# Computing the retention's k by features, with the weights standing, in a fused mixer and feed-forward kernel

## The chip, the cores and the metric

The kernel runs on one core of a Trainium2 chip. Its engines work side by side, each through its own queue in order: PE (TensorE, matrix products into the eight banks of PSUM), DVE (VectorE), ACT (ScalarE), POOL (GpSimd) and SP (SyncE, which issues most DMAs here). The metric is the device time of one execution in microseconds (us). The median of three executions of the kernel before is 429.26 us (429.15 to 429.53).

## The reference, cut to what matters

One layer of a model with 256 tokens of 1024 features. The input is modulated, `h = x * (1 + sc1) + sh1`, and one wide product makes every projection of the mixer:

```python
proj = h @ w_in
mq, mk, mv, rq, rk, rv, rg, g_a, g_r = jnp.split(proj, offsets, axis=-1)
mq = rotary_half(split_heads(mq, MOBA_HEADS), pos)
mk = rotary_half(split_heads(mk, MOBA_HEADS), pos)
y_a = moba_attention(mq, mk, split_heads(mv, MOBA_HEADS))
rq = retnet_rotate(split_heads(rq, RET_HEADS), pos)
rk = retnet_rotate(split_heads(rk, RET_HEADS), pos) * (RET_QK_DIM ** -0.5)
y_r = retention(rq, rk, split_heads(rv, RET_HEADS))
```

The retention has 4 heads of 128 features for q and k. Its rotation turns each pair of neighbouring features (2i, 2i+1) of a head by an angle that depends on the token:

```python
x0, x1 = xf[..., 0], xf[..., 1]
out = jnp.stack([x0 * cos - x1 * sin, x1 * cos + x0 * sin], -1)
```

Its scores are products of q and k over the 128 features of a head, so any order of these features does, if q and k have the same. After the mixer come two projections, a gate, an output projection, a layer norm, a feed-forward part with a short convolution, and a second layer norm.

## The kernel before, in words

PE works on numbers split into a high part (fp32r) and the rest, so that one product is three: high by high, high by low, low by high. Weights arrive from HBM as tiles of 128x2048 by SP's queue. Each half of such a tile, 128x1024, is split on the way: ACT copies it into `whi` (L1215) and DVE subtracts to make `wlo` (L1229). There are eight buffers of each.

The kernel begins with a phase A, which makes the modulated input `hh` (high) and `hl` (low, both by features: 128 features x 8 x 256 tokens) and, at the same time, the attention's q, k, v, the retention's q and one gate's first half, in all eight banks. `evac_A` (L966) moves these results out of the banks. Then comes a list of steps, one for each half tile of weights, carried out in order by the loop at the end of `_body`. In each step the loop first lets the side work go on (`run_sides`), then has the weights of up to six steps ahead split (`prep_to`), then carries out what was put off from an earlier step (`waiting`), and then issues the step's own matrix products. What stands in which order on an engine is settled by this loop when the program is written.

Three kinds of steps matter here. `xstat` (xh and xl stand in PE's array, the weights stream by): 12 products of 512 columns in a half tile, for two blocks of 128 tokens in two banks. Its result has tokens on the partitions. `wstat8m` (the weights stand, `hh` and `hl` side by side stream by): 8 products of 512 columns with `whi` (L116) and 8 of 256 columns with `wlo` (L118), into one bank; then ACT copies the bank's right half to SBUF (L448), and DVE, put off by one step, adds the left half to it (L451). Its result has features on the partitions. The third kind, `wstat4` and `wstat8`, also has weights standing.

The banks 0 to 3 go round: `two_banks` gives a pair in turn, `one_bank` the next one. Banks 4 to 7 belong to the side work: the attention and the retention.

The steps of the mixer are, in order: the retention's k (4 steps, `rk_done` L466), its v (8 steps), its gate (8), two other gates (4 and 8), two projections (4 and 8), then the output projection with banks 2, 3, 0, 1, 3 named in the code. Side by side with these, `mixers` (L980) ropes the attention's q and k (`rope`, L936, once for each block of tokens), turns them by features with PE's transposes and ACT's copies (`rot_T`, L957), and runs the attention head by head. It also ropes the retention's q and k, one of the four (block, q or k) per step (L1066), turns both by features (`rot_T`, L1072), and starts `retention` (L1074), which multiplies them (L1109, L1110).

## Time and profile before

| | |
|---|---|
| median of 3 executions | 429.26 us |
| the profiled execution, its own time | 428.88 us |
| its span in the profile | 427.2 us |
| PE busy | 415.9 us (97% of the span) |
| DVE busy | 373.4 us (87%) |
| ACT busy | 248.9 us (58%) |
| DMA, mean over the span | 247 GB/s |

The span is what the profile shows from the first to the last instruction; the execution's own time has 1.7 us around it. Busy shares are averages over the span. A matmul's end is modelled, so what a product costs is read from the distance between the starts of neighbours, not from its length.

### The profile page before, as it was taken

What the parts mean: (1) busy time and instruction counts of PE and PEld (TensorE: products, weight loads), DVE (VectorE), ACT (ScalarE), POOL (GpSimd) and SP (SyncE); (2) the same over time, 40 slices, a digit from 0 to 9 for tenths busy, and PEclk for the clock granted to TensorE, in tenths of its full rate; (3) what the DMA queues carried; (4) which work ended last, traced back from release to release, by engine and by line L of the source; (5) the groups of instructions that cost most, each with busy time, mean ns of one, the idle gap of its engine ahead of it and who ended that gap; (6) DMA issues with size and microseconds to landing.
All of it is one profiled execution on the core that took longest, in us unless ns stands there. A gap on an engine that the chain in (4) does not pass through costs nothing.

```text
span 427.2 us, 6209 instructions
## 1 busy us (share of the span) xinstructions
PE 415.9 (97%) x2316; PEld 357.2 (84%) x2316; DVE 373.4 (87%) x622; ACT 248.9 (58%) x404; POOL 7.3 (2%) x18
## 2 busy tenths in 40 slices
PE   6999999999999999999999999999999999999992
PEld 3888888877788998998889899888888888888882
DVE  5888999879997999999978887999999888789576
ACT  4667558779764488645543995654555545455400
POOL 0000000100000000001000000100000010000000
PEclk9999999999999999999999999999999999999998
DMA  7999988777468878789762075985875777550001
GB/s 261 407 412 396 399 284 358 275 291 298 164 242 327 284 262 297 296 295 353 283 202 98 2 275 219 348 288 192 296 276 216 292 284 235 189 192 1 2 25 74
DMA packets 19694, 105.61 MB, mean 247 GB/s; under 512 B 2640, under 2 KB 4560, under 8 KB 8912
## 3 DMA queue, kind: packets, MB, share of 16 engines
q1 hardware_dynamic: 18288, 100.23, 63.3%
q0 software_dynamic: 1376, 4.99, 3.3%
q8 instruction: 18, 0.29, 0.3%
q14 instruction: 12, 0.10, 0.1%
HBM read 104.15 MB, written 1.06 MB: 246 GB/s over the span
## 4 chain that ended last, share of the span: by engine, by line
PE 96%; DMA 1%; DVE 1%; SPq 1%; ACT 0%; issue 0%; DVEq 0%
PE P L116 22%; PE P L107 14%; PE P L108 13%; PE P L109 13%; PE P L118 12%; PE P L279 11%; PE P L289 3%; DMA raw<-in_strm 1%; PE P L674 1%; PE P L677 1%; PE P L676 1%; PE P L961 1%; PE P L1013 1%; PE P L1032 1%; PE P L1056 1%; PE P L1102 0%
## 5 line engine op out<-in xcount | busy, mean ns | idle before, releaser
L1229 DVE TENSOR_TENSOR wlo<-raw,whi 128x1024 fp32r<-128x1024 f32 x118 | 142.2, 1218 | 15.4 <-ACT whi L1215 15.0
L1215 ACT ACTIVATE whi<-raw 128x1024 fp32r<-128x1024 f32 x118 | 122.8, 1056 | 35.1 <-PE P L109 7.8
L206 DVE CUSTOM_DVE_ANT_0 junk<-raw,srow 128x1024 bf16<-128x1024 f32 x46 | 56.0, 1218 | 0.2
L116 PE MATMUL P<-AYa,whi 128*128 128x512 f32 x176 | 47.9, 394 | 0.0
L116 PE MATMUL P<-AYb,whi 128*128 128x512 f32 x176 | 47.2, 390 | 0.0
L107 PE MATMUL P<-whi,AH 128*128 128x512 f32 (+1 forms) x120 | 46.5, 388 | 0.0
L109 PE MATMUL P<-whi,AH 128*128 128x512 f32 (+1 forms) x120 | 45.2, 376 | 0.0
L108 PE MATMUL P<-wlo,AH 128*128 128x512 f32 (+1 forms) x120 | 45.1, 376 | 0.0
L116 PEld LDWEIGHTS P<-AYb,whi 128*128 128x128 f32 x176 | 33.0, 188 | 7.3
L448 ACT ACTIVATE A<-P 128x256 f32<-128x256 f32 x44 | 16.7, 380 | 34.9 <-PE P L118 32.9
L279 PE MATMUL P<-whi,AH 128*128 128x512 f32 x128 | 34.8, 394 | 0.4 <-ACT whi L263 0.4
L116 PEld LDWEIGHTS P<-AYa,whi 128*128 128x128 f32 x176 | 30.6, 190 | 4.3
L263 ACT ACTIVATE whi<-raw 128x1024 fp32r<-128x1024 f32 (+1 forms) x25 | 21.6, 883 | 17.6 <-DMA raw<-in_strm 16.4
L118 PEld LDWEIGHTS P<-AYa,wlo 128*128 128x128 f32 x176 | 26.9, 189 | 3.4
L266 DVE TENSOR_TENSOR wlo<-raw,whi 128x1024 fp32r<-128x1024 f32 (+1 forms) x25 | 24.6, 1010 | 5.3 <-ACT whi L263 5.1
L279 PEld LDWEIGHTS P<-whi,AH 128*128 128x128 f32 x128 | 23.5, 188 | 6.6 <-ACT whi L263 1.4
L118 PE MATMUL P<-AYb,wlo 128*128 128x256 f32 x176 | 28.3, 283 | 0.0
L118 PE MATMUL P<-AYa,wlo 128*128 128x256 f32 x176 | 28.0, 282 | 0.0
L107 PEld LDWEIGHTS P<-whi,AH 128*128 128x128 f32 x120 | 22.6, 188 | 5.0 <-issue 1.3
L109 PEld LDWEIGHTS P<-whi,AH 128*128 128x128 f32 x120 | 22.6, 188 | 4.3
L108 PEld LDWEIGHTS P<-wlo,AH 128*128 128x128 f32 x120 | 22.6, 189 | 3.6
L118 PEld LDWEIGHTS P<-AYb,wlo 128*128 128x128 f32 x176 | 24.3, 192 | 0.0
(277 smaller groups left out, 800.3 us busy)
## 6 DMA issues: line engine op xcount, KB each, us to landing
raw<-in_ada SPq DMA_DIRECT2D x16, 1024.0 KB, 5.5
raw<-in_wup SPq DMA_DIRECT2D x11, 1024.0 KB, 5.0
raw<-in_wgate SPq DMA_DIRECT2D x11, 1024.0 KB, 4.8
raw<-in_wdown SPq DMA_DIRECT2D x11, 1024.0 KB, 4.9
raw<-in_winB SPq DMA_DIRECT2D x10, 1024.0 KB, 6.9
raw<-in_strm SPq DMA_DIRECT2D x8, 1024.0 KB, 7.3
raw<-in_strm SPq DMA_DIRECT2D x12, 512.0 KB, 7.6
raw<-in_winGr SPq DMA_DIRECT2D x4, 1024.0 KB, 6.0
```

The costliest lines, as they stand in the source:

```text
L107: pe.matmul(o, lh, rh, start=start, stop=False)
L108: pe.matmul(o, lh, rl, start=False, stop=False)
L109: pe.matmul(o, ll, rh, start=False, stop=stop)
L116: pe.matmul(o, wh[:, k * 128:(k + 1) * 128], x2[k], start=k == 0, stop=False)
L118: pe.matmul(o[:, :256], wl[:, k * 128:(k + 1) * 128], x2[k][:, 0], start=False, stop=k == n - 1)
L206: dve.tensor_tensor_reduce(out=junk[:, rows], in0=raw[:, rows], in1=srow[:, rows], scale=1.0, scalar=0.0, op0=OP.mult, op1=OP.add, accum_o ...
L263: act.activation(hi[:, o], raw[:, o], AF.Copy)
L266: dve.tensor_tensor(lo[:, o], raw[:, o], f(hi[:, o]), OP.subtract)
L279: pe.matmul(pa[b0 + c // 512 * 2 + t], x[xi][:, j, t * 128:(t + 1) * 128], ws[k][:, c:c + 512], start=first and (xi, k) == (0, 0), stop=la ...
L448: act.activation(t, p[:, 256:], AF.Copy)
L1215: act.activation(hi, src, AF.Copy)
L1229: dve.tensor_tensor(lo, src, f(hi), OP.subtract)
```

## The change

The retention's k is made by two tiles of `wstat8m` in place of an `xstat`, from a weight tensor laid out for it (`winRk`). It is then by features from the start: for each head 128 features x 256 tokens, in the right half of the tiles `S["rqk", 0]` (heads 0 and 1) and `S["rqk", 1]` (heads 2 and 3). So k has four steps with one bank each (0, 1, 2, 3), and the turn of the banks comes out two banks on from there. Up to the first gate of the feed-forward part every step after k has the other pair of banks than before; at the first gate, `first` now sets the turn anew before the first half too, and from there the banks are the same as before.

The weights of the retention's q and k are permuted on the host within each head, even features first and then odd ones, so that the rotation's partners stand in two halves of 64 instead of side by side. `rope` loses its case for pairs: all ropes now use halves, the table of the sine has one half, and the sign is in a `scalar_tensor_tensor`. For k, features lie on partitions, so the partners lie 64 partitions apart: `k_swap` has ACT copy them across (two copies of 64x512 per block of two heads), and `k_rope`, one step later, does the rotation in three DVE instructions of 128x512 with a new table `kr` of 256 KB, loaded with the other constants. PE's transposes and ACT's copy for k are gone. In `mixers`, the attention's second block goes to banks 6 and 7 and not 4 and 5.

```diff
--- before.py
+++ after.py
...
-        for name, shape in (("cosm", [128, 2, 64]), ("sinm", [128, 2, 64]), ("mask", [128, 256]),
-                            ("cosr", [128, 2, 128]), ("sinr", [128, 2, 128]),
+        for name, shape in (("cosm", [128, 2, 64]), ("sinm", [128, 2, 32]), ("mask", [128, 256]),
+                            ("cosr", [128, 2, 128]), ("sinr", [128, 2, 64]),
                             ("convw", [128, 4, 22]), ("lncol", [128, 2, 8])):
             const(name, shape, sp)
+        consts["kr"] = slot("8b", [128, 4, 256])
+        sp.dma_start(consts["kr"][:, 0:2], a["kr"])
...
         def mk(half):
             def mm(hi, lo):
-                if half and mid:
-                    mid()
+                if mid:
+                    mid(half)
                 p = get()
...
-    def rk_done(bk):
-        for t in range(2):
-            act.activation(S["rqk", t][:, 512:1024], bk[t], AF.Copy)
-    xstat(None, "winB", 0, hh, hl, 8, lazy(two_banks), rk_done)
+    def rk_copy(half, u):
+        return S["rqk", u][:, 512 + half * 256:768 + half * 256]
+    for u in range(2):
+        wstat8m("winRk", u, lambda k: h1x2[:, :, k], lambda half, u=u: rk_copy(half, u), lambda half: None)
...
-        xstat(None, "winB", 2 + 2 * cc, hh, hl, 8, lazy(two_banks), rv_done)
+        xstat(None, "winB", 2 * cc, hh, hl, 8, lazy(two_banks), rv_done)
...
-        xstat(None, "winB", 6 + 2 * cc, hh, hl, 8, lazy(two_banks), rg_done)
+        xstat(None, "winB", 4 + 2 * cc, hh, hl, 8, lazy(two_banks), rg_done)
...
-    def first():
-        bank_i[0] = 0
-        up_T(1)
+    def first(half):
+        bank_i[0] = 2 - 2 * half
+        if half:
+            up_T(1)
     wstat8("wgate", 0, gh2, gl2, gate_done(0), first)
...
-    def rope(x, cos, sin, pairs):
-        n, w = cos.shape[-1], x.shape[-1]
-        heads = w // n
+    def rope(x, cos, sin):
+        w, h2, m = x.shape[-1], sin.shape[-1], cos.shape[-1]
+        n = 2 * h2
         t2 = slot("8a", [128, w])
-        hv = lambda t: t.rearrange("p (h n) -> p h n", n=n)
-        bc = lambda v, m: v.unsqueeze(1).to_broadcast([128, heads, m])
-        if pairs:
-            xv, tv = (hv(t).rearrange("p h (i two) -> p h i two", two=2) for t in (x, t2))
-            cv = sin.rearrange("p (i two) -> p i two", two=2)
-            for i in range(2):
-                dve.tensor_tensor(tv[:, :, :, i], xv[:, :, :, 1 - i], bc(cv[:, :, i], n // 2), OP.mult)
-        else:
-            h2 = n // 2
-            for i in range(2):
-                dve.tensor_tensor(hv(t2)[:, :, i * h2:(i + 1) * h2],
-                                  hv(x)[:, :, (1 - i) * h2:(2 - i) * h2],
-                                  bc(sin[:, i * h2:(i + 1) * h2], h2), OP.mult)
-        dve.tensor_tensor(hv(x), hv(x), bc(cos, n), OP.mult)
+        hv = lambda t, n: t.rearrange("p (h n) -> p h n", n=n)
+        bc = lambda v, k: v.unsqueeze(1).to_broadcast([128, w // k, v.shape[-1]])
+        for i in range(2):
+            o, y = hv(t2, n)[:, :, i * h2:(i + 1) * h2], hv(x, n)[:, :, (1 - i) * h2:(2 - i) * h2]
+            if i:
+                dve.tensor_tensor(o, y, bc(sin, n), OP.mult)
+            else:
+                dve.scalar_tensor_tensor(o, y, -1.0, bc(sin, n), op0=OP.mult, op1=OP.mult)
+        dve.tensor_tensor(hv(x, m), hv(x, m), bc(cos, m), OP.mult)
         dve.tensor_tensor(x, x, t2, OP.add)
+    def k_swap(x):
+        t2 = consts["kr"][:, 2:4].rearrange("p a b -> p (a b)")
+        for r in (slice(0, 64), slice(64, 128)):
+            act.activation(t2[r], x[64 - r.start:128 - r.start], AF.Copy)
+    def k_rope(x):
+        t = consts["kr"]
+        t2, xv = t[:, 2:4], x.rearrange("p (h t) -> p h t", h=2)
+        bc = lambda v: v.unsqueeze(1).to_broadcast([128, 2, 256])
+        dve.tensor_tensor(t2, t2, bc(t[:, 1]), OP.mult)
+        dve.tensor_tensor(xv, xv, bc(t[:, 0]), OP.mult)
+        dve.tensor_tensor(xv, xv, t2, OP.add)
...
-        roped = lambda i: rope(qk[i], consts["cosm"][:, i], consts["sinm"][:, i], False)
+        roped = lambda i: rope(qk[i], consts["cosm"][:, i], consts["sinm"][:, i])
...
-                    rot_T(qk[i - ROT_AT], i - ROT_AT, qkT, w, 4 + w)
+                    rot_T(qk[i - ROT_AT], i - ROT_AT, qkT, w, 4 + 2 * (i - ROT_AT) + w)
...
                 scores(i)
             if 0 <= i - RROPE < 4:
                 t, w = divmod(i - RROPE, 2)
-                rope(S["rqk", t][:, w * 512:w * 512 + 512], consts["cosr"][:, t], consts["sinr"][:, t], True)
+                x = S["rqk", t][:, 512:1024]
+                if w:
+                    k_rope(x)
+                else:
+                    rope(S["rqk", t][:, :512], consts["cosr"][:, t], consts["sinr"][:, t])
+                    k_swap(x)
             if 0 <= i - RROT < 2:
                 t = i - RROT
                 if t == 0:
-                    S["rT"] = [slot(n, [128, 4, 256]) for n in ("3a", "3b")]
-                for w in range(2):
-                    rot_T(S["rqk", t], t, S["rT"], w, 4 + 3 * w)
+                    S["rT"] = slot("3a", [128, 4, 256])
+                rot_T(S["rqk", t], t, [S["rT"]], 0, 4)
...
             if h < HR:
                 p = bank(4)
-                pe.matmul(p[:, 0:256], rT[1][:, h, 0:128], rT[0][:, h, :], start=True, stop=True)
-                pe.matmul(p[:, 256:384], rT[1][:, h, 128:256], rT[0][:, h, 128:256], start=True, stop=True)
+                o = 512 + h % 2 * 256
+                kr = S["rqk", h // 2][:, o:o + 256]
+                pe.matmul(p[:, 0:256], kr[:, 0:128], rT[:, h, :], start=True, stop=True)
+                pe.matmul(p[:, 256:384], kr[:, 128:256], rT[:, h, 128:256], start=True, stop=True)
...
-    cosm, sinm = lay(np.concatenate([c, c], 1)), lay(np.concatenate([-s, s], 1))
+    cosm, sinm = lay(np.concatenate([c, c], 1)), lay(s)
...
-    cosr, sinr = lay(np.repeat(c, 2, 1)), lay(np.stack([-s, s], -1).reshape(T, DK))
+    cosr, sinr = lay(np.tile(c, 2)), lay(s)
+    kr = np.stack([np.concatenate([c, c], 1).T, np.concatenate([-s, s], 1).T], 1)
...
-    return dict(cosm=cosm, sinm=sinm, cosr=cosr, sinr=sinr, decay=decay, mask=mask)
+    return dict(cosm=cosm, sinm=sinm, cosr=cosr, sinr=sinr, kr=kr, decay=decay, mask=mask)
...
-    wi = A(w_in)[0]
+    wi = A(w_in)[0].copy()
+    for c0 in (1536, 2048):
+        wi[:, c0:c0 + 512] = wi[:, c0:c0 + 512].reshape(-1, 4, 64, 2).transpose(0, 1, 3, 2).reshape(-1, 512)
...
-        winB=np.stack(sum([xs(wi, 2048 + 512 * i) for i in range(5)], [])),
+        winRk=np.stack([ws(wi, 2048 + 256 * i, 2) for i in range(2)]),
+        winB=np.stack(sum([xs(wi, 2560 + 512 * i) for i in range(4)], [])),
...
```

PE around the first step of the retention's v, before. P0 to P3 are banks of PSUM, `AH` holds `hh` and `hl`, `whi` and `wlo` are the split weights; the number behind a name tells one use of a buffer from the next.

```order
L108 MATMUL P1_718<-wlo_694,AH_123 128x512
L109 MATMUL P1_718<-whi_688,AH_123 128x512
L961 MATMUL P4_785<-ident_80,A2a_132 128x128 x4
L961 MATMUL P5_791<-ident_80,A2a_132 128x128 x4
L107 MATMUL P2_801<-whi_692,AH_123 128x512
L108 MATMUL P2_801<-wlo_700,AH_123 128x512
L109 MATMUL P2_801<-whi_692,AH_123 128x512
```

These are the last products of k (banks 0 and 1), the transposes of the attention's first block, and the first products of v, in bank 2, which nobody had used since phase A. The same place on PE in the changed kernel, from the first step of k:

```order
L116 MATMUL P0_719<-AH_123,whi_662 128x512 x8
L118 MATMUL P0_719<-AH_123,wlo_666 128x256 x8
L116 MATMUL P1_744<-AH_123,whi_664 128x512 x8
L118 MATMUL P1_744<-AH_123,wlo_670 128x256 x8
L116 MATMUL P2_767<-AH_123,whi_668 128x512 x8
L118 MATMUL P2_767<-AH_123,wlo_692 128x256 x8
L116 MATMUL P3_792<-AH_123,whi_690 128x512 x8
L118 MATMUL P3_792<-AH_123,wlo_696 128x256 x8
L974 MATMUL P4_810<-ident_80,A2a_132 128x128 x4
L974 MATMUL P5_816<-ident_80,A2a_132 128x128 x4
L107 MATMUL P0_827<-whi_694,AH_123 128x512
L108 MATMUL P0_827<-wlo_702,AH_123 128x512
```

The four steps of k now fill the banks 0 to 3 one after the other, and v's first product is in bank 0, the bank of k's first step. DVE in the same stretch of the program, before: `A2b` is the attention's second block, roped by L951 to L955, and the L1229 are the `wlo` of coming steps.

```order
L1229 TENSOR_TENSOR wlo_710<-raw_658,whi_702 128x1024
L951 TENSOR_TENSOR A8a_712<-A2b_133,sinm_644 128x16x32 x2
L954 TENSOR_TENSOR A2b_133<-A2b_133,cosm_642 128x1024
L955 TENSOR_TENSOR A2b_133<-A2b_133,A8a_712 128x1024
L1229 TENSOR_TENSOR wlo_733<-raw_658,whi_708 128x1024
L1229 TENSOR_TENSOR wlo_751<-raw_670,whi_731 128x1024
L1229 TENSOR_TENSOR wlo_767<-raw_670,whi_749 128x1024
```

And DVE there in the changed kernel, where L453 is the adding that frees a bank of k:

```order
L1248 TENSOR_TENSOR wlo_712<-raw_660,whi_704 128x1024
L952 SCALAR_TENSOR_TENSOR A8a_714<-A2b_133,sinm_644 128x16x32
L950 TENSOR_TENSOR A8a_714<-A2b_133,sinm_644 128x16x32
L953 TENSOR_TENSOR A2b_133<-A2b_133,cosm_642 128x1024
L954 TENSOR_TENSOR A2b_133<-A2b_133,A8a_714 128x1024
L1248 TENSOR_TENSOR wlo_739<-raw_660,whi_710 128x1024
L453 TENSOR_TENSOR AR0_675<-P0_719,AR0_675 128x256
L1248 TENSOR_TENSOR wlo_764<-raw_672,whi_737 128x1024
L453 TENSOR_TENSOR AR0_675<-P1_744,AR0_675 128x256
L1248 TENSOR_TENSOR wlo_787<-raw_672,whi_762 128x1024
```

The additions for banks 0 and 1 have come in behind the second block's rope and behind one and two more `wlo`; nothing else has moved in this stretch.

## Rows read from the trace of the kernel before

**Rows 1.** The page of the profile: the first line of its part 1 and the first line of its part 4 (the chain that ended last, by engine).

```profile
PE 415.9 (97%) x2316; PEld 357.2 (84%) x2316; DVE 373.4 (87%) x622; ACT 248.9 (58%) x404; POOL 7.3 (2%) x18
...
PE 96%; DMA 1%; DVE 1%; SPq 1%; ACT 0%; issue 0%; DVEq 0%
```

**Rows 2.** Who PE waited for in the whole span: us in total, times, longest.

```profile
PE P L191 <- DVE first L195: 3.2, 1, 3.2
PE P L279 <- ACT whi L263: 0.4, 1, 0.4
```

**Rows 3.** The timeline of PE from the first product of k: start, length, engine, line, operation, out<-in, count. L107 to L109 are an `xstat` step's products, L961 the transposes.

```profile
65.21 0.39 PE L107 MATMUL P<-whi,AH 128*128 128x512 f32 x1
...
75.86 0.39 PE L109 MATMUL P<-whi,AH 128*128 128x512 f32 x1
76.09 1.03 PE L961 MATMUL P<-ident,A2a 128*128 128x128 f32 x8
76.89 0.48 PE L107 MATMUL P<-whi,AH 128*128 128x512 f32 x1
...
78.34 0.39 PE L107 MATMUL P<-whi,AH 128*128 128x512 f32 x1
...
79.71 1.03 PE L961 MATMUL P<-ident,A2b 128*128 128x128 f32 x8
```

**Rows 4.** Pieces of the chain of waits in order of time: start, length, what. First the two groups of transposes of the retention's q and k (four of each in a group), then one half tile of a `wstat8m` step.

```profile
116.31 0.87 PE P L961 x8
...
121.22 0.87 PE P L961 x8
...
153.76 1.84 PE P L116 x8
155.60 0.95 PE P L118 x8
```

**Rows 5.** The timeline of DVE in the same stretch as rows 3: the first block's rope (L951 to L955, its middle left out), the `wlo` of coming steps, the second block's rope, and `wlo` again.

```profile
64.41 1.28 DVE L951 TENSOR_TENSOR A8a<-A2a,sinm 128x512 f32<-128x512 f32 x2
...
66.99 1.23 DVE L955 TENSOR_TENSOR A2a<-A2a,A8a 128x1024 f32<-128x1024 f32 x1
68.13 5.76 DVE L1229 TENSOR_TENSOR wlo<-raw,whi 128x1024 fp32r<-128x1024 f32 x5
73.81 1.28 DVE L951 TENSOR_TENSOR A8a<-A2b,sinm 128x512 f32<-128x512 f32 x2
...
76.39 1.23 DVE L955 TENSOR_TENSOR A2b<-A2b,A8a 128x1024 f32<-128x1024 f32 x1
77.53 5.76 DVE L1229 TENSOR_TENSOR wlo<-raw,whi 128x1024 fp32r<-128x1024 f32 x5
```

**Rows 6.** Groups of instructions by line and shape: count, busy us, mean ns of one, idle time before. L451 is the adding of a `wstat8m` step; L549 is a scalar_tensor_tensor with a number written in the instruction, L842 one with a scalar from a tile; L963 is ACT's copy of transposes.

```profile
L451 DVE TENSOR_TENSOR A<-P,A 128x256 f32<-128x256 f32 x44 | 18.3, 417 | 0.0
...
L549 DVE SCALAR_TENSOR_TENSOR A<-A2a,A8a 128x512 f32<-128x512 f32 x1 | 0.7, 693 | 0.0
L842 DVE SCALAR_TENSOR_TENSOR A7a<-A7a,sd,A 128x512 f32<-128x512 f32 x2 | 1.5, 740 | 0.0
L963 ACT ACTIVATE AYb<-P 128x512 f32<-128x512 f32 x4 | 2.5, 619 | 0.0
```

**Rows 7.** The timeline of ACT in the stretch of rows 3: the `whi` of coming steps, then one that waited for its weights.

```profile
66.66 6.88 ACT L1215 ACTIVATE whi<-raw 128x1024 fp32r<-128x1024 f32 x7
76.85 1.06 ACT L1215 ACTIVATE whi<-raw 128x1024 fp32r<-128x1024 f32 x1 [3.31 <-DMA raw<-in_winB]
```

**Rows 8.** The timeline of SP's queue: the last of the constants, and the next weights.

```profile
57.54 0.68 SPq L128 DMA_DIRECT2D lncol<-in_lncol  x1
61.51 11.60 SPq L96 DMA_DIRECT2D raw<-in_winB  x5
```

**Rows 9.** The timeline where the last `wstat8m` step of the mixer ends and the output projection begins: PE's last products of the former (four from 211.08 on), ACT's copy and DVE's adding that free its bank, and PE's first product for the second block of tokens.

```profile
211.08 0.64 PE L118 MATMUL P<-AYb,wlo 128*128 128x256 f32 x4
...
211.76 0.38 ACT L448 ACTIVATE A9b<-P 128x256 f32<-128x256 f32 x1 [0.94 <-PE P L118]
...
212.18 0.42 DVE L451 TENSOR_TENSOR A9b<-P,A9b 128x256 f32<-128x256 f32 x1
...
212.94 0.39 PE L107 MATMUL P<-whi,AH 128*128 128x512 f32 x1
```

**Rows 10.** Busy time of PE, PEld, DVE, ACT and POOL in three stretches, then the granted clock, the DMA share and GB/s: while ACT is fullest in the attention, and two stretches after PE's last matmul.

```profile
97.00:104.00 7.00, 7.00 (x39) 5.27 (x39) 6.86 (x22) 6.96 (x20) 0.00 (x0) 1.00 0.86 315
...
420.00:424.00 4.00, 0.00 (x0) 0.00 (x0) 3.86 (x11) 0.29 (x1) 0.00 (x0) 1.00 0.00 0
424.00:427.20 3.20, 0.00 (x0) 0.00 (x0) 0.37 (x1) 0.00 (x0) 0.00 (x0) 0.52 0.45 164
```

**Rows 11.** The timeline of PE at the start and the end of the kernel: its first eight transposes, the first product of phase A, and its last matmul.

```profile
3.23 1.94 PE L191 MATMUL P<-ident,sc 128*128 128x128 f32 x8 [3.23 <-DVE first L195]
...
8.85 0.50 PE L279 MATMUL P<-whi,AH 128*128 128x512 f32 x1 [0.42 <-ACT whi L263]
...
419.34 0.28 PE L109 MATMUL P<-whi,A 128*128 128x256 f32 x1
```

**Rows 12.** The timeline in the attention: ACT's copy of a head's transposed weights, and the products on PE that read it (of the pair's second head, in `A9b`).

```profile
109.20 0.49 ACT L1058 ACTIVATE A9b<-P 128x384 f32<-128x384 f32 x1 [0.89 <-PE P L1056]
...
111.86 0.43 PE L1032 MATMUL P<-A9b,A 128*64 128x256 f32 x1
```

## The prediction

> **What bounds the kernel now.** I read the page first: PE is busy 97% of the span and the chain that ended last is 96% PE [rows 1]. Then the view of waits, for PE alone: apart from the very start PE waited for nobody [rows 2]. So the time is the sum of what PE does, one thing after the other, plus a head and a tail. Whatever ACT, DVE and the DMAs do is free as long as PE finds its operands and an empty bank ready, and a new wait of PE counts in full. Two questions follow: how much PE work goes or comes, and whether PE, which waits nowhere now, will wait somewhere. For the second I read the timelines of PE, DVE and ACT side by side in the stretch where the change puts new instructions [rows 3, 5, 7].
>
> **PE's work.** k before: from 65.21 to 76.09, 10.88 us for 48 products [rows 3]. k after is four half tiles of a form that the kernel has elsewhere: 1.84 for eight products of 512 columns and 0.95 for eight of 256, so 2.79 a half [rows 4], 11.16 us in all. That is 0.28 more. The retention's transposes come in two groups of 0.87 for eight [rows 4]; half of each goes, 2 x 0.435 = 0.87 less. If nothing waited the sum would be 0.28 - 0.87 = -0.59 us.
>
> **The bank that v finds.** This is the step on which I rest the forecast. Before, v's first product went to bank 2, empty since phase A. After, it goes to bank 0, which held k's first half and is free only when ACT has copied its right half and DVE has added its left half. The copy is early: ACT has it behind the first five of the seven `whi` from 66.66 on, 0.98 us each, so at about 71.6, and k's first step on PE ends by 65.21 + 2.79 = 68.0 [rows 3, 7]. The addition is late. It stands on DVE behind the second block's rope and one more `wlo`, as the order shows, and DVE has no slack there: its instructions follow one another without a gap from 64.41 to 83.3 [rows 5]. So:
> - The second block's rope ended at 76.39 + 1.23 = 77.62, and the next `wlo` began at 77.53, since neighbours overlap a little [rows 5]. Two multiplications of 128x512, one per block, become scalar_tensor_tensors with a number in the instruction: 693 ns, against 1.28 for two of the old kind, whose single lengths with the overlap are some 0.68. I take +0.01 each; 740 ns is the other end, +0.06 each [rows 5, 6]. The `wlo` now begins at 77.55.
> - A `wlo` takes 5.76 / 5 = 1.15 from start to start [rows 5]: the addition for bank 0 begins at 78.70 and, at 417 ns [rows 6], ends at 79.12.
> - PE is at v's first product at 76.89 + 0.28 = 77.17 [rows 3]. It waits until 79.12 plus about 0.04 for the signal, which is what lay between a `whi` done and its first product at 8.85 [rows 11]; so 79.16, or 2.27 later than before.
> - The addition for bank 1 stands one `wlo` further on: 79.12 - 0.07 (overlap) + 1.15 + 0.42 = 80.62, or 80.69 without the overlap. PE's six products in bank 0 take 6 x 10.88 / 48 = 1.36 from 79.16, until 80.52. So PE waits again, by 0.1 to 0.2, and begins in bank 1 at about 80.7, where it began at 78.34 [rows 3].
> PE leaves this step 2.35 us later than before. The 0.28 of k's longer products lies inside that. Behind the waiting product on PE stand the rest of the step, the second block's transposes and all that follows; nobody ahead of PE makes it up, since PE was the bound already. The additions for banks 2 and 3 end some 3 us after that, and v comes to these banks only four steps on.
>
> **What else moves, and why I take it at nothing.** The four additions (1.67 us of DVE) delay the `wlo` of coming steps. But by 77.9 eleven `whi` have been made (three before evac_A, seven, and one) while PE begins its fifth half tile [rows 3, 7]: the weights are six steps ahead, and PE never waited for them [rows 2]. If that cover were gone it would cost the 1.67. `kr` adds 256 KB on SP's queue and the smaller tables take 96 KB off. SP was idle from 58.2 to 61.51, between the last constant and the next weights [rows 8], so the extra issue fits; 160 KB more at the page's mean of 247 GB/s is 0.65 us, and the `whi` that waits for its DMA until 76.85 [rows 7] is the eleventh, needed six steps later. `k_swap` gives ACT four copies of 64x512; the nearest row is 619 ns for 128x512 [rows 6], so 1.2 us in each of two steps, less two copies of transposes. They fall where ACT is 6.96 of 7.00 busy [rows 10]; I come back to this below. The ropes of q and k on DVE come out even: three instructions of 128x512 for k in place of four. The products of the retention itself keep their count and shape. In the output projection, bank 3 is now the bank of the last `wstat8m` half; the same copy and addition ended at 212.60 and PE came to its second bank at 212.94 [rows 9]. A slack of 0.3 us, so nothing to 0.1. The attention's second block in banks 6 and 7 can only remove a wait, and PE had none. From the feed-forward part on the banks are the same.
>
> **Sum.** +2.35 at v's first step, -0.87 of transposes: +1.48 us. Against the profiled execution's 428.88 that is 430.4; this execution lay 0.38 below the median of the runs shown, 429.26, so for the median I say 430.7.
>
> **Rivals.**
> 1. *The bank is free in time.* Then only PE's work counts: 429.26 - 0.59 = 428.7, not slower. Its place is the same addition, and it decides at PE's arrival, 77.17: DVE would have to be done with it 1.95 us earlier than by its rows. For it speaks only that the left half could be read early; against it that the order puts the addition behind a full row of work that cannot be shortened. 7 in 100.
> 2. *The clock falls while PE waits.* After PE's last matmul, at 419.6, the granted clock still read 1.00 up to 424 and 0.52 behind it [rows 10, 11]: of 2.4 GHz it fell to 1.2 only after an idle time of more than 4 us, and a wait of 2 us is shorter. At the start the low level shows in the transposes, 1.94 for eight against 1.03 [rows 3, 11], and PE's work from 3.23 to 8.85 would bound how long it stays low: half of 5.6 is 2.8 us more, 433.5. 5 in 100. The Trainium skill (TensorE: Matmul & The Clock Gate, section "A second HAM failure mode: psum-queue depth-cycling") says that PE pausing between groups of products, because of the turn of PSUM buffers, can make the clock swing between its two levels and cost throughput beyond the pauses. By that rule this would be the case to lose more than the wait; the trace has no pause of that kind in the middle, and its only row on the matter, the tail, speaks against it for a single pause.
> 3. *ACT or DVE run late in the attention.* The two copies of `k_swap` stand ahead of a `whi` and the next step's exponentials. If PE had to wait for them in full in both steps, that is 2 x 1.2 = 2.4 us, 433.1. But the narrowest place I find, a head's copy ended at 109.69 and read by PE at 111.86, has 2.2 us [rows 12], and ACT was waiting 0.89 just before that copy. PE is also 2.35 us later from the first wait on, which only helps. A part of it, up to 1 us, is the likelier form: 431.7. 9 in 100.
>
> **How the numbers follow.** The forecast case has 79 in 100, with its own range from 430.0 (DVE's stretch 0.5 us shorter than I count, and PE's gain a little larger) to 431.4 (740 ns for the new form, 0.3 at the output projection, a later signal). With the milder part of rival 3 I give 430.0 to 431.7 for 8 in 10. A difference of 0.2%, 0.86 us here, is about what a measurement of this kernel can tell from no change: slower begins at 430.12, faster ends at 428.40. The forecast case and the rivals 2 and 3 are slower, but for a low edge of the first, 0.88; rival 1 lies within 0.2%, and with that edge I give 0.09; faster would need rival 1 and some gain that I don't see, 0.03.
>
> **What would show it.** In the changed profile's waits, PE at L107 waiting for DVE's L453 (the addition on `AR`), twice, about 1.9 to 2.0 and 0.1 to 0.2 us. PE's first product of v at 79.1 to 79.2, where L118's last of k ends by 76.4. Groups of four transposes at the retention's two places, 0.43 each, and PE's busy share lower by about the wait. I am wrong if PE shows no wait there, if it is longer than 3 us, if the clock drops behind it, or if a second wait of more than 0.3 us stands in the attention or at the output projection.

## The result and the profile after

The changed kernel took 431.48 us (median of 7 executions, 430.88 to 433.66), the kernel before 429.4 beside it (429.15 to 430.4): a ratio of 1.0056, 95% interval 1.0042 to 1.007. The prediction was 430.7, range 430.0 to 431.7. The direction was right and the loss too small: +1.48 us was forecast, and +2.1 came, +2.4 by the ratio. This median lies inside the range, near its upper end. Two later sets of the same kernel on other occasions gave still more: 432.49 against 429.62 (1.0068, 1.005 to 1.0085) and 433.89 against 429.65 (1.0088, 1.0062 to 1.0114), and their medians lie 0.8 and 2.2 above the range.

The profiled execution of after took 431.52 us, its span is 429.8 (before: 428.88 and 427.2). First the page, the lines that answer to [rows 1], then PE's waits, which answer to [rows 2]:

```profile
PE 416.1 (97%) x2324; PEld 357.0 (83%) x2324; DVE 374.8 (87%) x624; ACT 250.6 (58%) x408; POOL 7.3 (2%) x18
...
PE 74%; DMA 11%; DVE 6%; ACT 5%; issue 2%; SPq 1%; DVEq 0%; ACTq 0%
```

```profile
PE P L193 <- DVE first L197: 3.2, 1, 3.2
PE P L107 <- DVE AR L453: 2.0, 1, 2.0
PE P L281 <- ACT whi L265: 0.7, 1, 0.7
PE P L281 <- ACT AH L250: 0.2, 1, 0.2
PE P L1069 <- ACT A9a L1071: 0.2, 1, 0.2
```

PE's busy share reads 97% as before, and says nothing. The chain does: it was 96% PE, and 22% of it now runs over DMAs, DVE and ACT. In the waits two rows are new behind the first stage: L107 for DVE's addition L453, the wait that the prediction rests on, and a small one for ACT, L1069.

PE's timeline, which answers to [rows 3] (L116 and L118 are a half of k, L974 the transposes, L107 to L109 v's products):

```profile
65.72 1.98 PE L116 MATMUL P<-AH,whi 128*128 128x512 f32 x8
...
76.87 1.04 PE L974 MATMUL P<-ident,A2a 128*128 128x128 f32 x8
79.86 0.50 PE L107 MATMUL P<-whi,AH 128*128 128x512 f32 x1 [1.95 <-DVE AR L453]
...
81.35 0.47 PE L107 MATMUL P<-whi,AH 128*128 128x512 f32 x1
...
82.81 1.03 PE L974 MATMUL P<-ident,A2b 128*128 128x128 f32 x8
```

And DVE's, which answers to [rows 5]:

```profile
62.74 1.28 DVE L986 TENSOR_TENSOR A2a<-P,A2a 128x512 f32<-128x512 f32 x2
...
68.86 5.76 DVE L1248 TENSOR_TENSOR wlo<-raw,whi 128x1024 fp32r<-128x1024 f32 x5
74.53 0.69 DVE L952 SCALAR_TENSOR_TENSOR A8a<-A2b,sinm 128x512 f32<-128x512 f32 x1
...
77.11 1.22 DVE L954 TENSOR_TENSOR A2b<-A2b,A8a 128x1024 f32<-128x1024 f32 x1
78.25 1.22 DVE L1248 TENSOR_TENSOR wlo<-raw,whi 128x1024 fp32r<-128x1024 f32 x1
79.39 0.42 DVE L453 TENSOR_TENSOR AR<-P,AR 128x256 f32<-128x256 f32 x1
79.72 1.22 DVE L1248 TENSOR_TENSOR wlo<-raw,whi 128x1024 fp32r<-128x1024 f32 x1
```

The two read together: PE has the transposes behind it at 77.9 and stands still until DVE, which has not had a free moment since 62.74, has done the second block's rope, one `wlo` and the addition. How much later PE is than before, at the same place of the program: 0.51 at k's start, 0.78 at its end (76.09 to 76.87), 2.97 at v's first product, 3.1 at the second transposes (79.71 to 82.81), 2.21 after both groups of the retention's transposes, which are four instead of eight, and 2.75 from 128 us on. The last step up, 0.54, is a loss that the sum had put at nothing, and PE's timeline shows it where the retention begins (L1056, then L1069, are the last head's transposes, L1109, then L1128, the retention's first product). Before and after:

```profile
124.47 0.39 PE L109 MATMUL P<-whi,AH 128*128 128x512 f32 x1
124.70 0.49 PE L1056 MATMUL P<-ident,A 128*128 128x128 f32 x3
125.03 0.60 PE L1109 MATMUL P<-AYa,AYb 128*128 128x256 f32 x2
...
125.60 0.48 PE L107 MATMUL P<-whi,AH 128*128 128x512 f32 x1
```

```profile
126.64 0.39 PE L109 MATMUL P<-whi,AH 128*128 128x512 f32 x1
127.19 0.55 PE L1069 MATMUL P<-ident,A 128*128 128x128 f32 x3 [0.16 <-ACT A9a L1071]
127.68 0.70 PE L1128 MATMUL P<-AYa,AR 128*128 128x256 f32 x2
...
128.35 0.48 PE L107 MATMUL P<-whi,AH 128*128 128x512 f32 x1
```

The transposes come 0.55 behind the start of the product ahead of them, where before it was 0.23, and from them to the next step's first product it takes 1.16, where before it was 0.90. What PE waits for is ACT, in ACT's timeline:

```profile
104.66 1.27 ACT L960 ACTIVATE A8b<-AR 64x512 f32<-64x512 f32 x2
...
113.74 1.28 ACT L960 ACTIVATE A8b<-AR 64x512 f32<-64x512 f32 x2 [0.64 <-DVE AR L968]
...
123.02 1.06 ACT L1234 ACTIVATE whi<-raw 128x1024 fp32r<-128x1024 f32 x1 [1.93 <-DMA raw<-in_winGa]
124.09 1.28 ACT L487 ACT_TABLE_LOAD   x1
...
126.62 0.51 ACT L1071 ACTIVATE A9a<-P 128x384 f32<-128x384 f32 x1
```

L960 are `k_swap`'s copies. The gate's weights were issued at 118.22, where before it was 114.18: 4.0 later, while PE was only some 3 later. SP's queue, before and after:

```profile
114.18 0.33 SPq L96 DMA_DIRECT2D raw<-in_winGa  x1
```

```profile
118.22 0.33 SPq L96 DMA_DIRECT2D raw<-in_winGa  x1
```

### The profile page after: what moved, and what is told of

Its sections match the earlier page's. It is cut to its first block, busy times and chain, and to the rows that moved or that the text cites. A ratio compares the mean times of both kernels' runs of the same rounds, so it can differ in the third digit from the quotient of the medians.

```text
span 429.8 us, 6226 instructions
## 1 busy us (share of the span) xinstructions
PE 416.1 (97%) x2324; PEld 357.0 (83%) x2324; DVE 374.8 (87%) x624; ACT 250.6 (58%) x408; POOL 7.3 (2%) x18
## 3 DMA queue, kind: packets, MB, share of 16 engines
HBM read 104.32 MB, written 1.06 MB: 245 GB/s over the span
## 4 chain that ended last, share of the span: by engine, by line
PE 74%; DMA 11%; DVE 6%; ACT 5%; issue 2%; SPq 1%; DVEq 0%; ACTq 0%
PE P L116 22%; PE P L118 12%; PE P L107 11%; PE P L108 11%; PE P L109 11%; DMA raw<-in_strm 8%; DVE wlo L1248 1%; DMA raw<-in_winB 1%; DVE wlo L268 1%; ACT whi L265 1%; DMA raw<-in_winGa 1%; ACT whi L1234 1%; PE P L677 1%; PE P L680 1%; PE P L679 1%
## 5 line engine op out<-in xcount | busy, mean ns | idle before, releaser
L116 PE MATMUL P<-AYa,whi 128*128 128x512 f32 x176 | 47.9, 394 | 0.0
L116 PE MATMUL P<-AYb,whi 128*128 128x512 f32 x176 | 47.2, 390 | 0.0
L107 PE MATMUL P<-whi,AH 128*128 128x512 f32 (+1 forms) x104 | 40.4, 388 | 2.0 <-DVE AR L453 2.0
L116 PEld LDWEIGHTS P<-AYb,whi 128*128 128x128 f32 x176 | 33.0, 188 | 7.3
L109 PE MATMUL P<-whi,AH 128*128 128x512 f32 (+1 forms) x104 | 38.9, 374 | 0.0
L108 PE MATMUL P<-wlo,AH 128*128 128x512 f32 (+1 forms) x104 | 38.9, 374 | 0.0
L116 PEld LDWEIGHTS P<-AYa,whi 128*128 128x128 f32 x176 | 30.6, 190 | 4.3
L118 PEld LDWEIGHTS P<-AYa,wlo 128*128 128x128 f32 x176 | 26.9, 189 | 3.4
L281 PEld LDWEIGHTS P<-whi,AH 128*128 128x128 f32 x128 | 23.5, 188 | 7.2 <-ACT whi L265 1.8
L118 PE MATMUL P<-AYb,wlo 128*128 128x256 f32 x176 | 28.3, 283 | 0.0
L118 PE MATMUL P<-AYa,wlo 128*128 128x256 f32 x176 | 28.0, 282 | 0.0
L107 PEld LDWEIGHTS P<-whi,AH 128*128 128x128 f32 x104 | 19.6, 188 | 6.7 <-DVE AR L453 2.4
L118 PEld LDWEIGHTS P<-AYb,wlo 128*128 128x128 f32 x176 | 24.3, 192 | 0.0
L116 PE MATMUL P<-AH,whi 128*128 128x512 f32 x96 | 24.2, 394 | 0.0
L109 PEld LDWEIGHTS P<-whi,AH 128*128 128x128 f32 x104 | 19.6, 188 | 3.6
```

What stands on the lines that cost most here:

```text
L107: pe.matmul(o, lh, rh, start=start, stop=False)
L108: pe.matmul(o, lh, rl, start=False, stop=False)
L109: pe.matmul(o, ll, rh, start=False, stop=stop)
L116: pe.matmul(o, wh[:, k * 128:(k + 1) * 128], x2[k], start=k == 0, stop=False)
L118: pe.matmul(o[:, :256], wl[:, k * 128:(k + 1) * 128], x2[k][:, 0], start=False, stop=k == n - 1)
L281: pe.matmul(pa[b0 + c // 512 * 2 + t], x[xi][:, j, t * 128:(t + 1) * 128], ws[k][:, c:c + 512], start=first and (xi, k) == (0, 0), stop=la ...
```

## The experiments

### The kernels once more

`again` and `again2` are the changed kernel, `before_again` is the kernel before.

> The changed kernel as it is, profiled and timed once more. First theory on the 0.5 us that the stage before k added (k's first product at 65.72 us instead of 65.21, with the same code ahead of it): it is scatter of that stage's transfers from run to run. Then the start of k moves by a few tenths between profiles of one kernel, and may come at 65.2 here. Rival: the change brings it (other transfers, other places in memory), and k starts at 65.6 to 65.8 again. For the time both expect 431.5 us, 430.9 to 433.7 in single runs.

Measured: 432.49 us (432.3 to 433.38), k's first product at 65.38.

> The kernel before, profiled once more, to see whether VectorE's row of additions at the end of the first stage stands at 62.0 us there as in the first profile, or moves. In the four profiles of changed kernels so far it begins at 62.7 to 63.3. Theory (scatter of that stage's transfers): it comes between 61.9 and 63.3 here, and k's first product at 65.2 to 65.9. Rival (the change brings it): 62.0 and 65.2 again. In both the product of v waits for nothing and the time is 428.7 to 430.9 us.

Measured: 430.45 us in its one execution. DVE's additions began at 63.75 (62.01 in the first profile of before) and k's first product at 65.91. In the timeline of PE, before then had a wait of its own, which the first profile did not have, and lost 0.9 there:

```profile
81.18 1.14 PE L961 MATMUL P<-ident,A2b 128*128 128x128 f32 x8 [0.62 <-ACT AYa L963]
```

So the first stage does scatter, in both kernels, and by more than was expected: 63.75 is 0.45 beyond the latest that the expectation had allowed. Over all 14 profiles of this study, whose first stage is the same code but for the tables among the constants, k's first product began between 65.15 and 66.22, with a median of 65.44; DVE's first addition of that stage's end between 62.01 and 63.75, with a median of 63.1. The profile on which the prediction rests had the earliest DVE of all.

`again` showed something else. In PE's timeline the products behind the pause are longer:

```profile
79.86 0.50 PE L107 MATMUL P<-whi,AH 128*128 128x512 f32 x1 [2.29 <-DVE AR L453]
80.20 0.48 PE L108 MATMUL P<-wlo,AH 128*128 128x512 f32 x1
80.48 0.63 PE L109 MATMUL P<-whi,AH 128*128 128x512 f32 x1
...
83.84 0.40 PE L108 MATMUL P<-wlo,AH 128*128 128x512 f32 x1
```

The busy times by stretch say why (the columns as in [rows 10]; the granted clock is the number ahead of the last two). First the profile of after, then `again`:

```profile
78.00:80.00 2.00, 0.14 (x1) 0.14 (x2) 2.00 (x4) 2.00 (x4) 0.71 (x1) 1.00 0.24 54
80.00:82.00 2.00, 2.00 (x9) 1.50 (x10) 2.00 (x3) 0.17 (x1) 0.00 (x0) 1.00 0.83 286
82.00:84.00 2.00, 2.00 (x15) 1.75 (x14) 2.00 (x4) 0.56 (x2) 0.00 (x0) 1.00 1.13 340
```

```profile
78.00:80.00 2.00, 0.14 (x1) 0.14 (x2) 2.00 (x4) 1.99 (x4) 0.59 (x1) 1.00 0.44 134
80.00:82.00 2.00, 2.00 (x6) 1.57 (x7) 2.00 (x3) 0.00 (x0) 0.00 (x0) 0.59 0.78 239
82.00:84.00 2.00, 2.00 (x6) 1.56 (x6) 2.00 (x4) 0.00 (x0) 0.00 (x0) 0.56 1.01 397
84.00:86.00 2.00, 2.00 (x15) 1.74 (x14) 1.33 (x2) 1.06 (x3) 0.35 (x1) 1.00 0.93 389
```

A granted clock of 0.5 is 1.2 of 2.4 GHz. PE started anew at the same 79.86 in both, but in `again` it was 1.5 later than after by 84 us, because the clock had fallen. That is rival 2, which the first profile had not shown. That profile does show that the row at the kernel's end, on which the prediction had set the rival aside, was one draw among many. In before the clock held for 4.5 us behind the end of the last product; in after it fell within 2 us:

```profile
422.08 0.28 PE L109 MATMUL P<-whi,A 128*128 128x256 f32 x1
```

```profile
424.00:426.00 2.00, 0.00 (x0) 0.00 (x0) 1.97 (x6) 0.29 (x1) 0.00 (x0) 0.57 0.00 0
```

### The banks of k

```diff
-                p = one_bank()
+                p = bank(at[half]) if at else one_bank()
...
+                ((2, 6), (7, 3))[u])
...
-                    rot_T(qk[i - ROT_AT], i - ROT_AT, qkT, w, 4 + 2 * (i - ROT_AT) + w)
+                    rot_T(qk[i - ROT_AT], i - ROT_AT, qkT, w, 4 + w)
```

> The changed kernel with k's four half products in banks 2, 6, 7 and 3 instead of 0 to 3, and the second pair of transposes back in banks 4 and 5: v's first pair 0 and 1 is then free from 64 us on. Theory (the wait for bank 0, 1.95 us, and the one for bank 1 behind it, 0.08, go into the end in full): the PE row that waits for DVE's addition is gone, and the time falls by 2.0, from 431.5 to 429.5 us. First rival (ScalarE and VectorE, late in the attention, set the pace anyway, and PE would only wait there instead): the wait at 79.9 us goes, the wait near 127 us grows from 0.54 to 1.5 or more, and the time falls by 1.0 or less, to 430.5 us or above. Second rival (another bank waits in its place, since k's halves now stand in the attention's banks): a new wait of 1 to 2 us between 68 and 90 us, and the time stays at 431 us.

Measured: 429.23 us (428.81 to 430.17), 0.9991 of the kernel before (0.998 to 1.0002), and 3.3 below `again` beside it. The wait is gone, and no other has come between 68 and 90 us; in PE's timeline v follows the transposes at once:

```profile
76.53 1.04 PE L975 MATMUL P<-ident,A2a 128*128 128x128 f32 x8
77.33 0.48 PE L107 MATMUL P<-whi,AH 128*128 128x512 f32 x1
```

k began at 65.39, as in `again` (65.38), so the two profiles can be set beside each other: the span is 427.1 against 431.2, and of these 4.1 PE has 2.5 at v's first product and 1.6 in the products behind it. The wait goes into the end in full, and with it what the clock took. Near 125 us PE still lost 0.47 here.

### The addition one place earlier, and one step later

`early` moves k's additions ahead of their step's `wlo` on DVE; `putoff2` puts them off by two steps.

```diff
-                put_off(1, rest)
+                (early if name == "winRk" else waiting).append((S["main"] + 1, rest))
...
+        while early and early[0][0] <= s:
+            early.pop(0)[1]()
         prep_to(max(need) + 1, True)
```

> The changed kernel with k's additions ahead of the subtraction of their step on VectorE instead of behind it: the first comes 1.14 us earlier, at 78.3 us, and the wait of PE for bank 0 falls to 0.8 to 1.3 us. Theory (time by the wait's length, and by the clock that falls behind the longer pauses): v's first product at 78.7 us, the granted clock stays 1.00 from 77 to 86 us, and the time falls by 1.14 from the runs without a fall (431.7), to 430.5 us, with single runs within 1 us of each other. Rival (the clock falls whatever the length of the wait): the median falls by 1.14 only from 432.4, to 431.3 us, and some profiles and runs still have 1.5 us more.

> The changed kernel with k's additions put off by two steps instead of one, so that VectorE has one more subtraction of 1.13 us (and the next addition's place) ahead of the first: it comes some 1.46 us later, and the wait of PE for bank 0 becomes about 3.4 to 3.9 us. Theory (PE waits by VectorE's clockwork alone, and what follows a pause of this length is a stretch of about 4 us at the lower clock level, granted 0.50 to 0.56, which costs 1.5 us more): PE goes on at 81.3 us, the granted clock falls in the profile and in nearly all runs, and the median is 1.5 above the longer runs of the changed kernel, 434.5 to 435 us. Rival (the falls of the clock at 80 us in two of three profiles have nothing to do with the pause's length): the clock falls in some runs only, and single runs spread from 433 to 434.7 us.

```diff
-                put_off(1, rest)
+                put_off(2 if name == "winRk" else 1, rest)
```

Measured: `early` 431.02 us (430.33 to 432.77), the clock 1.00 from 76 to 88 us in its profile; `putoff2` 435.38 (433.8 to 436.78), the clock 0.60 and 0.55 from 80 to 84. The two rows of PE's timelines, `early` first:

```profile
79.36 0.50 PE L107 MATMUL P<-whi,AH 128*128 128x512 f32 x1 [1.72 <-DVE AR L453]
```

```profile
80.50 0.77 PE L107 MATMUL P<-whi,AH 128*128 128x512 f32 x1 [2.97 <-ACT whi L1234]
```

`early` was forecast with a pause of 0.8 to 1.3 and v at 78.7, and had 1.72 and 79.36. The step of 1.14 was there, but from a later start: DVE's first addition stood at 63.38. Its time lies between the 430.5 and the 431.3 that were expected and settles nothing between them. Its single runs spread by 2.4 us and not by 1, so more than this profile shows happens in some of them. In `putoff2` the row names a `whi` on ACT, which ended at 80.48; DVE's addition had ended at 80.35, so up to 0.1 of the pause is ACT's. Its v came only 0.64 later than in after, since its DVE began at 62.14, the second earliest of all; counted from there it is 1.24, against 1.46 forecast.

All kernels with the pause, by their profiles (us; the clock is that granted from 82 to 84):

| kernel | DVE's first addition | v's first product | apart | pause named | clock |
|---|---|---|---|---|---|
| after | 62.74 | 79.86 | 17.12 | 1.95 | 1.00 |
| again | 62.74 | 79.86 | 17.12 | 2.29 | 0.56 |
| again2 | 63.70 | 80.82 | 17.12 | 2.41 | 0.50 |
| dveswap | 62.87 | 79.98 | 17.11 | 2.38 | 0.69 |
| filler | 63.51 | 80.63 | 17.12 | 1.20 | 1.00 |
| early | 63.38 | 79.36 | 15.98 | 1.72 | 1.00 |
| putoff2 | 62.14 | 80.50 | 18.36 | 2.97 | 0.55 |

The fourth column is the point: in the five kernels with the same order on DVE, v begins 17.11 to 17.12 us after DVE's first addition, so it begins when DVE has gone through a fixed row of work. PE's own start of k, which lay between 65.34 and 66.22 in these profiles, changes nothing in that.

### The pause filled

```diff
+                if i == ROT_AT:
+                    p = bank(6)
+                    for _ in range(8):
+                        pe.matmul(p, hh[:, 0, 0:128], hh[:, 0:2].rearrange("p a b -> p (a b)"),
+                                  start=True, stop=True)
```

> The changed kernel with eight products of 128x512, which nothing reads, into bank 6 behind the first transposes: PE works for 8 x 0.23 = 1.84 us of the time in which it would stand still before v's first product, and the wait for bank 0 stays what VectorE makes it. Theory (what comes on top of the wait in some runs is the lower clock level behind a pause of more than about 2 us): v's first product at 79.9 us as before, a remaining idle of 0.1 to 0.7, the granted clock 1.00 from 76 to 88 us, and the median falls from that of the changed kernel beside it (432.4 in both sets so far) by about 0.7, to that of its runs without a fall, 431.6 us. Rival (the clock falls there for another reason, or the fall costs the median nothing): median as the changed kernel's, or the clock low again at 80 us.

> The changed kernel once more, beside the one with the pause filled, on the same chip: 431.5 to 432.5 us by both theories. If the pause before v's first product is over 2.2 us in the profile, the theory of the clock expects a granted clock of 0.5 to 0.6 from 80 to 84 us; if it is under 2.0 us, 1.00.

Measured: `filler` 433.54 us (433.47 to 433.82), `again2` 433.89 (431.67 to 435.17). The clock behaves as the theory has it: 1.00 throughout with the pause filled, 0.50 behind the 2.41 of `again2`, and the runs of `filler` lie within 0.35 us of each other where those of `again2` spread by 3.5. The median does not: it should have been 431.6. In `filler` v began at 80.63, 0.7 above the forecast's 79.9, and PE lost 1.8 near 125 us instead of 0.5, since there the gate's weights landed 6.1 us after their issue (4.8 in after). ACT's timeline shows what that cost it:

```profile
125.11 1.06 ACT L1239 ACTIVATE whi<-raw 128x1024 fp32r<-128x1024 f32 x1 [3.23 <-DMA raw<-in_winGa]
```

So the fall makes the changed kernel's runs spread; what it adds to the median is not shown by this. Why the weights were slow here is not settled either.

The granted clock averaged over each run's span, which the record has for every run, says more. Of the 19 runs of the changed kernel in its three sets, the nine at 0.994 or above took 430.88 to 432.38 us, with a median of 431.5, and the ten at 0.993 or below 432.12 to 435.17, with a median of 433.5. Of these ten, two are among the seven of the first set, three among the six of `again` and five among the six of `again2`, which is the order of the three medians. Where PE has no pause, in `banks`, the clock orders nothing: its three runs at 0.994 or below took 428.9 to 429.8, the others 428.81 to 430.17. The average also counts the clock behind the last product, which costs nothing, so it can't show where in a run the clock fell.

### ScalarE's copies of the partners

Five kernels take them away. `dveswap` and `both` (with the banks turned) let DVE multiply across the halves of the partitions:

```diff
-            act.activation(t2[r], x[64 - r.start:128 - r.start], AF.Copy)
...
-        dve.tensor_tensor(t2, t2, bc(t[:, 1]), OP.mult)
+        for r, o in ((slice(0, 64), slice(64, 128)), (slice(64, 128), slice(0, 64))):
+            sn = t[o, 1].unsqueeze(1).to_broadcast([64, 2, 256])
+            dve.scalar_tensor_tensor(t2[r], xv[o], -1.0, sn, op0=OP.mult, op1=OP.mult)
```

> The changed kernel with the four copies of ScalarE for k's partners gone: VectorE multiplies the partners across the two halves of the partitions itself, in two instructions of 64x512 instead of one of 128x512. ScalarE loses 4 x 0.63 = 2.5 us between 104 and 115 us and no longer waits for the one partner buffer (0.64); VectorE gets one instruction more for each token half, some 0.7 us each. The wait for bank 0 stays. Theory (the loss of 0.54 us at 127 us comes from ScalarE, made late by those copies): PE loses 0.1 or less there, and the time falls by 0.5, to 431.0 us. Rival (that loss has another cause, VectorE's work or the load of the gate's weights): PE still loses 0.4 to 0.6 there and the time stays at 431.5 us, or rises by up to 0.7 with VectorE's longer work.

> The two edits together: k's halves in banks 2, 6, 7 and 3, and the partners multiplied by VectorE without ScalarE's copies. Theory (the wait for bank 0 and ScalarE's lateness are the two losses, and they add): 431.5 - 2.0 - 0.5 = 429.0 us, which is 0.4 below the kernel before (429.4), the 0.59 of PE work that the change saves less what the first stage scatters. Rival (they are one loss: once PE no longer waits at 79.9, ScalarE's lateness has another size): no better than the edit of the banks alone, 429.5 us.

Measured: `dveswap` 432.88 us (431.52 to 435.1), `both` 428.8 (428.55 to 429.8), 0.9985 of before (0.9974 to 0.9995), which is not clear of the banks alone. Near 125 us PE lost 0.37 and 0.36, not 0.1. That much of the theory fell. Two instructions of 64x512 take DVE 1.39 where one of 128x512 took 0.69, so DVE now brought the delay that ScalarE had brought, which the runs further down bear out.

`banks_dma` swaps by transfers on POOL's queue, with the banks turned:

```diff
-            act.activation(t2[r], x[64 - r.start:128 - r.start], AF.Copy)
+            nc.gpsimd.dma_start(t2[r], x[64 - r.start:128 - r.start])
```

> The banks edit (k's halves in banks 2, 6, 7, 3) and the swap of k's partners by two transfers on the queue of POOL for each token half, in place of the two copies of ScalarE. VectorE's work is that of the changed kernel (0.69 for the one multiplication of 128x512), ScalarE loses 4 x 0.63 = 2.5 us. In the edit of the banks alone PE loses 0.47 us near 125 us behind ScalarE's copies (VectorE waits 1.06 for ScalarE at 107 us, the load of the gate's weights is issued 1.37 late); with VectorE's own swap it lost 0.36, where VectorE had 0.7 us more work for each token half. Theory (each of the two lost there by its own engine's extra work, and with none on either engine the loss goes): PE loses 0.1 or less near 125 us, and the time is 0.4 below the edit of the banks alone: 428.8 us, 0.7 to 0.9 below the kernel before. Rival (the loss comes from k's rope being in another place, or the transfers come late and VectorE waits for them): 0.3 to 0.5 lost again, 429.2 us or above.

Measured: 430.27 us (428.71 to 431.09), worse than the banks alone; PE lost 1.2 near 125 us. The time was the rival's, the way was not: DVE waited for no transfer. POOL's queue was empty, so the first pair went out at 82.58, into the fullest stretch of the weights; it took 9.2 us to land, and ACT stood still for weights issued right behind it, 4.67 against 1.54 with the banks alone:

```profile
92.53 1.06 ACT L1235 ACTIVATE whi<-raw 128x1024 fp32r<-128x1024 f32 x1 [4.67 <-DMA raw<-in_winB]
```

`banks_noswap` leaves the copies out and puts nothing in their place:

```diff
-        dve.tensor_tensor(t2, t2, bc(t[:, 1]), OP.mult)
+        dve.tensor_tensor(t2, xv, bc(t[:, 1]), OP.mult)
...
-                    k_swap(x)
```

> The banks edit with k's partner copies left out and nothing in their place: k is multiplied by its own rows where the partners belong, so the retention's result is another one, but VectorE's instructions, shapes and order are those of the edit of the banks, and no transfer is added. Theory (with the banks turned, what PE still loses near 125 us, 0.47, is ScalarE's copies, which hold up L87's copy and with it VectorE by 1.06, and so the gate's weights): VectorE waits 0.2 or less there, PE loses 0.1 or less at 125 us, and the time is 0.4 below that of the banks alone: 428.8 us. Rival (the loss comes from the transfers' scatter in that stretch, as it did when two more transfers were put there): 0.3 or more lost, 429.2 us or above.

Measured: 428.44 us (428.13 to 429.24), 0.9972 of before (0.9962 to 0.9982). PE loses nothing near 125 us. From the last head's transposes to the next step's product it is 0.90 again, as before the change:

```profile
123.98 0.49 PE L1065 MATMUL P<-ident,A 128*128 128x128 f32 x3
...
124.88 0.47 PE L107 MATMUL P<-whi,AH 128*128 128x512 f32 x1
```

With the copies in, DVE shows the way they take, in its timeline of `banks`:

```profile
107.18 0.42 DVE L88 TENSOR_TENSOR A<-P,A 128x256 fp32r<-128x256 f32 x1 [1.06 <-ACT A L87]
```

ACT, with 1.27 us of copies ahead, comes to L87 at 106.78, where before it was 105.06; DVE waits 1.06 for it; and the `wlo` that frees the buffer for the gate's weights comes later too: they are issued at 115.55, before at 114.18 and in `banks_noswap` at 114.29. DVE's own swap does the same by its length: in `both` they are issued at 115.84, 1.55 later than in `banks_noswap`, though its k began only 0.71 later.

`banks_sp` makes the swap by transfers on SP's queue, between the loads of weights, with the banks turned.

```diff
-            act.activation(t2[r], x[64 - r.start:128 - r.start], AF.Copy)
+            sp.dma_start(t2[r], x[64 - r.start:128 - r.start])
...
-                    k_swap(x)
+            if i in (RROPE - 1, RROPE + 2):
+                k_swap(S["rqk", (i - RROPE + 1) // 3][:, 512:1024])
```

> The banks edit, and k's partners swapped by two transfers of 128 KB on SP's queue for each token half, between the loads of weights (the first pair behind the load issued at 97 us in the edit of the banks, the second behind that of 105.8 us), in place of ScalarE's copies: the result is the reference's, no engine has more work than in the kernel whose copies were left out. Theory (the copies of ScalarE are the whole of what PE still lost near 125 us): PE loses 0.1 or less there and the time is that of the kernel without the swap, 0.28% below the kernel before: 428.4 us, about 0.8 below the edit of the banks alone. Rival (the transfers hold the loads of weights up, as the ones on POOL's queue at 82.6 us did, or land late, and VectorE waits for them): VectorE or ScalarE waits 1 us or more for a transfer between 100 and 118 us, and the time is 429.2 us or above.

Measured: 428.56 us (428.38 to 429.24), 0.998 of before (0.9969 to 0.9991). PE loses nothing near 125 us, nobody waits for a swap, and the gate's weights are issued at 115.25 in a profile whose k began 0.8 later than before's. SP's queue:

```profile
98.86 1.56 SPq L961 DMA_DIRECT2D A8b<-AR  x2
...
110.76 1.11 SPq L961 DMA_DIRECT2D A8b<-AR  x2
115.25 0.33 SPq L96 DMA_DIRECT2D raw<-in_winGa  x1
```

This version is faster than both kernels: 0.7 us below before, where the changed kernel is 2.1 to 4.2 above it. It differs from `banks_dma` in the queue and in the place of the transfers at once, so which of the two makes them harmless is not separated.

## Why the prediction fell short

- **PE's work** was right. k's four halves took 76.87 - 65.72 = 11.15 us (11.16 forecast), and each group of transposes gave back 0.43 to 0.45.
- **The bank that v finds** was right in its mechanism: the wait is L107 for L453, with about 0.1 more at bank 1, and turning the banks takes it away. PE's row reads 1.95 at bank 0, counted from a modelled end; from start to start, as the forecast was, it is 79.86 - 77.67 = 2.19 against 1.99, since DVE was 0.70 later than forecast and PE 0.50. The multiplication with a number in the instruction took 0.68 to 0.69, so its price was right too.
- **The term that was mis-sized is v's start, 79.16.** It was worked out from DVE's row in one profile, where DVE began at 62.01, the earliest of 14. By the table v begins 17.12 us after that row begins: 62.01 + 17.12 is 79.13, so the row itself was sized well; for the median of 63.1 it is 80.2. I had shifted the sum by the 0.38 by which the profiled run lay below the median, as if all terms moved alike. But the wait ties PE to DVE, whose start is 1.1 later in the median than in that profile, while PE's own, k's, is 0.2 later. In the profile of after this is 0.70 of the difference (79.86 against 79.16). With the 0.54 of the next point the forecast's 1.48 becomes 2.72; in the two profiles the last product came 2.74 later (419.34 and 422.08). That the first set's median still fell inside the range is owed to the room left for rival 3, not to the terms of the sum.
- **`k_swap`, put at nothing, cost 0.5: rival 3 in its mild form, at 9 in 100.** I had looked for PE's narrowest place behind ACT and found 2.2 us of slack [rows 12]. The copies' delay came out elsewhere: by DVE, the issue of the gate's weights, their `whi` and a table load, to PE 20 us later. It is 0.54 in the profile of after and 0.47 with the banks turned; `banks_noswap` shows that it is the copies. My argument that PE, being later from the first wait on, would only be helped by that was wrong: DVE and ACT were later too.
- **Rival 2 came in some runs, at 5 in 100.** My ground against it, that the clock had held for 4 us behind the last product [rows 10, 11], did not carry over: it fell behind pauses of 2.29 to 2.97 in four profiles and held behind 1.20 to 1.95 in three. That row came from one execution; behind the last product the clock held for 4.5 us in before, but for 1.8 in after, 2.5 in `both` and 5.1 in `banks`. The price at the place is 1.4 to 1.5 us (4.37 to 4.44 from v's first product to the second transposes, against 2.95 after), not 2.8. The 2.8 had no row of the clock behind it: I took the length of the first transposes for the low level, and the granted clock reads 1.00 there, from 3 to 11 us. The Trainium skill (TensorE: Matmul & The Clock Gate, section "A second HAM failure mode: psum-queue depth-cycling") speaks of short pauses that PSUM banks, cycled through in each iteration, put between groups of products, and of a clock that swings for it at a cost in throughput. These profiles agree as to the cost, 1.4 to 1.5 us, though here it took a single pause.
- Left open: why the clock fell in more runs of one set than of another, by which the three sets lie at 2.1, 2.9 and 4.2 above before. The nine runs at the higher average lie about 2 above before, the other ten about 4; the 2 between them are more than the price of one fall, and no trace shows the rest.

## What to carry to other kernels

A PSUM bank is free only when its last reader has come round in its own queue: before turning banks anew, look at what stands ahead of that reader, not at how long it reads. A wait that ties the bounding engine to another one makes it inherit that engine's scatter, so size it from several profiles and not from one. And a copy put on a side engine that has no slack shows up where its delay has travelled to, here two engines, one transfer and 20 us on. A transfer of the same bytes in its place cost nothing between the loads on SP's queue, and about 1 us, by the medians, on POOL's queue in the fullest stretch of the loads.

## What the hardware showed that I had not expected

- Behind one pause of PE of 2.29 to 2.97 us in the middle of the kernel the granted clock read 0.50 to 0.69 from 82 to 84 us, and 1.00 again from 86. Behind the last product of the kernel it held for 1.8 to 5.1 us in the 14 profiles.
- Half the partitions cost as much as all: a copy of 64x512 took ACT 632 ns (619 for 128x512, from PSUM), a multiplication of 64x512 took DVE 0.69 (0.68 for 128x512).
- Two transfers of 128 KB each, sent out at 82.58 into a full stretch (DMA share 0.94 from 82 to 84), took 9.2 us to land; the four that went out at 98.9 and 110.8 took 6.0 in the median, and nobody waited for them.
